# A two-layer encoder on one core: second score products with 128 rows, and a static order made with other costs

## The chip, the core and the metric

The kernel runs on one core of one Trainium2 chip. The metric is the device time of one execution, in microseconds. Three executions of the kernel before were timed; the table further down has them. The profile is of one more execution.

The engines are named as in the profile: PE is TensorE (PEld its weight loads), DVE is VectorE, ACT is ScalarE, POOL is GpSimd, SP is SyncE, which issues the loads and stores.

## The reference

256 tokens of width 1024 pass two layers and a final RMSNorm, all in float32. Cut to what matters:

```python
def hybrid_layer(x, ...):
    proj = rmsnorm(x, n1) @ w_in                       # 1024 -> 2304
    qa, ka, va, qb, kb, vb = jnp.split(proj, cuts, axis=-1)
    qa = axial_rope(rmsnorm(qa, q_norm), ...)          # A: 8 heads of q, 2 of k and v
    ka = axial_rope(rmsnorm(ka, k_norm), ...)
    ya = global_gqa(qa, ka, va)                        # softmax over all 256 keys
    yb = dilated_window_attention(partial_rope(qb), partial_rope(kb), vb)   # B: 8 heads
    y = jnp.concatenate([rmsnorm(ya, out_norm_a), rmsnorm(yb, out_norm_b)], axis=-1)
    x = x + y @ w_out
    u = jnp.square(jax.nn.relu(rmsnorm(x, n2) @ w_mlp_in))   # 1024 -> 4096
    return x + u @ w_mlp_out
```

A head has 64 dims. The three dilated patterns of B merge, on 256 tokens, into one softmax with a mask of logarithms.

## The kernel before, in words

**Products in two parts.** Each float32 operand is split into a part `hi`, rounded to the format that TensorE reads in one pass, and the rest `lo`. A product is then three: hi·hi, hi·lo and lo·hi. The weights come by DMA into a ring `wraw` of 4096 columns (`dma_more`, L468), are split into the rings `whi` and `wlo` of 8192 columns, in pieces of up to 640 (`prep_piece`, L476; `hi` on ACT or DVE, `lo` on DVE, or on DVE or POOL for the weights ahead of the MLP), and are used in the order in which TensorE takes them (`plan`, L35).

**A layer.** q and k of A come first (120 products of 256 columns). Then come the V products (96 of 320 columns), and between them the column sums and transposes that k's and q's norms need (`hook_a0` to `hook_a4`, L676 to L726). The constants in `tabt` (rotary tables, mask) are loaded behind the first weights. Then the 16 heads are run (`score`, `turn`, `pv`, L793 to L840), and the products that don't need them stand between: q and k of B (`fill_pair`, L754) and the A half of the output projection (`fill_wa`, L764). The B half (`fill_wb`), B's norm (`ynorm_col`, `rowbc`), the residual, the second norm and the MLP follow. In layer 1 the sums of the last product start from x, transposed (`seed`, L1002).

**A head's scores** (`score`). q of a head is stationary: its 64 rows of `hi`, and in the other 64 partitions the 64 rows of its `lo`. k's `hi` stands twice, on both halves, so one product of 128 rows gives (q_hi + q_lo)·k_hi. A second product adds q_hi·k_lo, and takes the 64 rows of q_hi alone:

```python
mm(b[:, th], q[:, th * 128:(th + 1) * 128], ks[0], True, False)
mm(b[:, th], q[a, th * 128:(th + 1) * 128], ks[1][a], False, True)
```

This is done for both halves `th` of the tokens: four products of 256 columns a head, 128 in all, 64 of them with 64 rows. In the profile and in the order they are the products that read `qs`, with `ka` for the heads of A and `kbt` for those of B. Behind the scores come, on DVE, the row maximum and small instructions on two numbers a partition (`hst`), on ACT the exponential, and on POOL, DVE or ACT the division by the sum (`pr`); then TensorE transposes `pr` into `h` and `l`, which the P·V products take.

**What sets the order.** Every instruction is recorded by `Sequencer` (L136) and issued from one line, L368, in a static order. `cost` (L191) gives each an assumed duration. `record` (L220) marks which instructions take the SBUF port that DVE and POOL share: DVE's with two SBUF operands, or of the copy and scale kinds from SBUF to SBUF, and POOL's that read SBUF. `order` (L261) is a list schedule over these costs, and `justify` moves all as late, then as early as it can be. `issue` (L361) runs it twice: first with the port, which settles on which engine each instruction runs, then again with engines fixed, and this pass gives the order. In the second pass the marks of the port are left out:

```python
# once with the shared port, for the choice of engines, and once without
self.order()
self.ops = [([x for x in o[0] if x[0] == e], *o[1:5], {}, *o[6:]) for o, e in zip(self.ops, self.on)]
for i in self.order():
```

On the chip each engine keeps its own order and waits on semaphores for the others' results.

Of the kernel before, what the change touches and what calls it, by code (L numbers as in the profile page):

```python
# [10 lines left out]
F32 = mybir.dt.float32  # L11
# [8 lines left out]
NRAW = 4096     # columns of weights as they come  # L20
NHI = 8192      # and split
# [6 lines left out]
NIN0 = 3                              # pairs of ff blocks in the K-outer start of the MLP  # L28
LAG = 2
N_PAIR = 16  # L30
# what an engine's end counts more, in the choice among several, per kind of instruction
# [3 lines left out]
def plan():  # L35
    """The weights in chunks of some columns, in the order in which TensorE takes them."""
    out = []
# [15 lines left out]
def lay_weights(w_in, w_out, w1, w2):  # L53
    """The weights as TensorE takes them: rows of 128 on the partitions, columns
    in the heads' order (kv0 with kv1, first with second of a pair)."""
# [52 lines left out]
def tables():  # L108
    """Constants that depend on shapes alone: rotary cosines and signed sines on
    [dim of two heads, token], the logarithms (times 8) of how many of the dilated  # L110
    patterns a key is in, the identity, and sums over a head or all."""
# [24 lines left out]
class Sequencer:  # L136
    """Takes a kernel's instructions in program order, keeps what that order says
    of their data, and issues them in the order of a list schedule: each engine takes,
    of what is ready for it, what has the longest way to the end."""

    # from the end of one engine's instruction to the start of another's that waits for it
# [21 lines left out]
    def form(e, method, args, kw):  # L163
        """An engine's instruction for what several engines can do."""
# [12 lines left out]
    def regions(ap, psum):  # L177
        """Where an access lies: partitions and spans of the free axis (a whole PSUM bank)."""
# [12 lines left out]
    def cost(e, method, outs, ins, kw):  # L191
# [6 lines left out]
        if e == "PE":  # L198
            f32 = ins[0].dtype == F32
            if kw.get("is_transpose") or method == "transpose":  # L200
                return 109
            return max(110, 1.7 * n) if f32 else max(109, 0.423 * n)
# [17 lines left out]
    def record(self, engines, method, args, kw):  # L220
# [28 lines left out]
        if engines == ("SP",):  # L249
            # the loads in program order  # L250
            if self.last is not None:
                deps.setdefault(self.last, False)
            self.last = i
        # the SBUF port that DVE and Pool share
# [6 lines left out]
    def order(self):  # L261
# [31 lines left out]
        while done < n:  # L293
# [10 lines left out]
            if len(ops[i][0]) > 1:  # L304
                # the engine that ends it first
# [20 lines left out]
    def justify(self, start, end, succ):  # L326
        """Moves all instructions as late as they may be, then as early: gaps close."""
# [3 lines left out]
        for back in (True, False):  # L331
            busy = {e: [] for e in (*self.eng, "PORT")}     # spans, counted from this pass's beginning
# [28 lines left out]
    def issue(self):  # L361
        # once with the shared port, for the choice of engines, and once without
        self.order()
        self.ops = [([x for x in o[0] if x[0] == e], *o[1:5], {}, *o[6:]) for o, e in zip(self.ops, self.on)]
# [15 lines left out]
def trunk(ctx: ExitStack, tc: tile.TileContext, x, wts, prm, tab, fin, out):  # L380
# [19 lines left out]
    # ---------------------------------------------------------------- tiles  # L400
# [21 lines left out]
    KA = [[T(f"ka{i}{s}", [128, S], F32R) for s in range(2)] for i in range(2)]  # L422
# [3 lines left out]
    tq = T("tq", [128, 2, S])             # gain-folded sines of q and k  # L426
    tb = T("tb", [128, 2, S])             # rs-folded tables of B
# [16 lines left out]
    # ------------------------------------------------------------- weights  # L444
# [6 lines left out]
    def places(total):  # L451
        """Each chunk's place in a circular buffer, and the last chunk that it overwrites."""
# [23 lines left out]
    def prep_piece():  # L476
        """Splits a piece of the next chunk, if its place is free."""
# [27 lines left out]
    def wgt(key, a, n, last=True):  # L505
        """(hi, lo) of n columns from a on in a chunk; with `last`, their last use."""
# [17 lines left out]
    # --------------------------------------------------------- small pieces  # L524
    def col(src, rhs, n, o):
        """o[token, th, n] <- column sums of src [128, 256] (weights rhs)."""
        for th in range(2):
            mm(o[:, th], src[:, th * 128:(th + 1) * 128], rhs, True, True)

    def rowbc(c2, o):  # L530
        """o [128, 256] <- c2 [token, th] along the free axis on every partition."""
# [8 lines left out]
    def sums(l, ps):  # L540
        """From column sums of squares of x: mean square + eps, and its power -1/2."""
# [11 lines left out]
    # ---------------------------------------------------------------- start  # L553
    DVE.memset(ssx[:, 0:128], 0.0)
    # TensorE's clock rises while it waits for x
# [10 lines left out]
    DVE.memset(one, 1.0)  # L566
    x3 = x.rearrange("p (a b) -> p a b", a=KB)
# [46 lines left out]
    def norm_x(l):  # L614
        """norm's scale along the tokens, from the squares' sums."""
# [8 lines left out]
    # ---------------------------------------------------------------- layer  # L624
    for l in range(L):
        gA, gA2, gK, gK2 = P(l, 16), P(l, 17), P(l, 18), P(l, 19)
        # gain-folded tables
# [3 lines left out]
        # ---- q and k of A, K-outer behind the split of h  # L631
# [7 lines left out]
        # ---- V of all heads, tokens on the partitions, with the rest of A's q, k between  # L639
# [17 lines left out]
        def k_split(kh, kst_):  # L657
            """kst_[head][hi, lo]: each a head's 64 rows twice."""
# [15 lines left out]
        cq = cqt.rearrange("p (t h) -> p t h", t=2)   # scale of q's scores / 8  # L674
# [78 lines left out]
        # ---- attention of the 16 heads, with the products that don't need it between  # L753
# [324 lines left out]
```

## Time and profile before

| | |
|---|---|
| timed executions | 629.90, 632.05, 635.52 us; median 632.05 |
| span of the profiled execution | 630.3 us (no other time of that execution is known) |
| layer 0: A's q, k and V | to 46.2 us |
| layer 0: 16 heads | 46.2 to 122.0 us |
| layer 0: rest of the projection, second norm | to about 147 us |
| layer 0: MLP | to about 330 us |
| layer 1: 16 heads | 350.8 to 426.2 us |
| layer 1: MLP | from about 458 us |
| DMA | 98.58 MB, mean 156 GB/s |
| mean granted clock of TensorE | 0.992 |

All instructions are recorded by one helper and stand at L368, so the profile is read by tiles: `bank` is PSUM; `whi`, `wlo` the split weights; `hh`, `hl` the normed x; `h`, `l` the transposed softmax or the MLP's inner layer; `sm` and `hst` small columns; `f` scratch. Before the bar of a group's row stand the instruction, its shape and its count; behind it the busy us and the mean ns of one; then the engine's idle time before it. In a timeline's row stand the start, the us from first start to last end, the engine and the instruction with its count. Matmuls overlap each other in the array: what one costs is read from start to start.

### The profile page before, as it was taken

The numbers are of one execution on the slowest core, as the hardware profiler recorded it, in microseconds if no ns is written. First come the engines' busy times: TensorE is split into PE (matmuls) and PEld (weight loads), VectorE is DVE, ScalarE is ACT, GpSimd is POOL, SyncE is SP. The second block draws the span as 40 slices with busy tenths as digits, with TensorE's granted clock in tenths as the row PEclk, the third lists the DMA queues.
The fourth block names the chain that finished last, engine by engine and source line by source line (L and its number), as shares of the span: only waits on it lengthen the run. The fifth ranks groups of instructions, "written<-read, shape, count | busy, mean of one in ns | idle before, by whom it ended". The sixth has DMA issues, their size and how long they took to land.

```text
span 630.3 us, 11899 instructions
## 1 busy us (share of the span) xinstructions
PE 611.6 (97%) x4500; PEld 576.6 (91%) x4500; DVE 483.9 (77%) x873; ACT 353.4 (56%) x723; POOL 181.9 (29%) x179
## 2 busy tenths in 40 slices
PE   8989999989999999999999999999999999999996
PEld 8988987989999999999999888898989999999995
DVE  6898899998986566666588879887988766667632
ACT  6567877865544444434464687786654444434412
POOL 1486885841000000000035766667300000000000
PEclk9979999999999999999999999999999999999999
DMA  7833111346674554645444301025568554544501
GB/s 262 275 150 134 68 68 34 130 139 201 251 251 167 203 186 151 222 177 178 141 151 134 135 35 68 34 74 173 158 242 297 204 205 156 221 180 149 186 1 67
DMA packets 29865, 98.58 MB, mean 156 GB/s; under 512 B 3440, under 2 KB 3952, under 8 KB 29808
## 3 DMA queue, kind: packets, MB, share of 16 engines
q1 hardware_dynamic: 29808, 97.82, 44.3%
q8 instruction: 35, 0.57, 0.3%
q14 instruction: 22, 0.18, 0.1%
HBM read 96.76 MB, written 1.05 MB: 155 GB/s over the span
## 4 chain that ended last, share of the span: by engine, by line
PE 65%; DVE 11%; issue 2%; ACT 1%; POOL 1%; POOLq 0%; ACTq 0%; DVEq 0%
PE bank L368 65%; DVE wlo L368 2%; DVE f L368 2%; DVE hl L368 2%; DVE qs L368 1%; DVE hst L368 1%; DVE xT L368 1%; DVE l L368 1%; DVE pr L368 1%; DVE kbt L368 0%; POOL sm L368 0%; ACT f L368 0%; ACT pr L368 0%; POOL f L368 0%; DVE yA__82 L368 0%
## 5 line engine op out<-in xcount | busy, mean ns | idle before, releaser
L368 ACT ACTIVATE whi<-wraw 128x640 fp32r<-128x640 f32 (+3 forms) x312 | 192.9, 643 | 171.3 <-PE bank L368 113.0
L368 DVE TENSOR_TENSOR wlo<-wraw,whi 128x640 fp32r<-128x640 f32 (+3 forms) x296 | 221.0, 777 | 64.7 <-ACT whi L368 63.5
L368 PE MATMUL bank<-hh,whi 128*128 128x256 f32 x784 | 222.4, 285 | 0.7 <-ACT whi L368 0.7
L368 PE MATMUL bank<-hl,whi 128*128 128x256 f32 x784 | 222.5, 285 | 0.6 <-DVE hl L368 0.5
L368 PE MATMUL bank<-hh,wlo 128*128 128x256 f32 x784 | 221.2, 285 | 0.1
L368 PEld LDWEIGHTS bank<-hh,whi 128*128 128x128 f32 x784 | 149.2, 191 | 2.4 <-ACT whi L368 1.2
L368 PEld LDWEIGHTS bank<-hl,whi 128*128 128x128 f32 x784 | 148.1, 189 | 1.4 <-DVE hl L368 1.2
L368 PEld LDWEIGHTS bank<-hh,wlo 128*128 128x128 f32 x784 | 147.3, 189 | 0.6 <-DVE wlo L368 0.3
L368 POOL TENSOR_TENSOR wlo<-wraw,whi 128x384 fp32r<-128x384 f32 (+1 forms) x49 | 66.8, 1375 | 161.1 <-DMA wraw<-in_w_dram 149.7
L368 PE MATMUL bank<-l,whi 128*128 128x256 f32 x256 | 72.4, 283 | 0.0
L368 PE MATMUL bank<-h,wlo 128*128 128x256 f32 x256 | 72.2, 282 | 0.0
L368 PE MATMUL bank<-h,whi 128*128 128x256 f32 x256 | 71.3, 280 | 0.0
L368 POOL TENSOR_TENSOR sm<-sm,mhalf 128x2 f32<-128x2 f32 (+2 forms) x12 | 11.8, 986 | 183.8 <-DVE sm L368 183.8
L368 PE MATMUL bank<-wlo,h 128*128 128x512 f32 (+1 forms) x160 | 56.1, 350 | 0.0
L368 PE MATMUL bank<-whi,l 128*128 128x512 f32 (+1 forms) x160 | 55.9, 349 | 0.0
L368 PE MATMUL bank<-whi,h 128*128 128x512 f32 (+1 forms) x160 | 55.8, 349 | 0.0
L368 PEld LDWEIGHTS bank<-h,whi 128*128 128x128 f32 x256 | 48.4, 190 | 0.0
L368 PEld LDWEIGHTS bank<-h,wlo 128*128 128x128 f32 x256 | 48.0, 188 | 0.0
L368 PEld LDWEIGHTS bank<-l,whi 128*128 128x128 f32 x256 | 47.9, 187 | 0.1
L368 POOL TENSOR_TENSOR ssx<-ssx,f 128x512 f32<-128x512 f32 (+1 forms) x22 | 27.6, 1253 | 48.7 <-ACT f L368 37.3
L368 ACT ACTIVATE h<-f 128x512 fp32r<-128x512 f32 x32 | 20.2, 631 | 28.1 <-DVE f L368 28.1
L368 DVE CAST whi<-wraw 128x640 fp32r<-128x640 f32 (+1 forms) x33 | 14.8, 452 | 26.9 <-PE bank L368 25.6
(113 smaller groups left out, 994.8 us busy)
## 6 DMA issues: line engine op xcount, KB each, us to landing
wraw<-in_w_dram SPq DMA_DIRECT2D x148, 512.0 KB, 3.7
wraw<-in_w_dram SPq DMA_DIRECT2D x31, 320.0 KB, 3.3
wraw<-in_w_dram SPq DMA_DIRECT2D x16, 384.0 KB, 3.3
tabt<-in_t_dram SPq DMA_DIRECT2D x1, 768.0 KB, 7.5
xT<-in_x_dram SPq DMA_DIRECT2D x1, 512.0 KB, 7.0
tabt<-in_f_dram SPq DMA_DIRECT2D x1, 512.0 KB, 7.0
out_dram<-f SPq DMA_DIRECT2D x1, 512.0 KB, 2.6
out_dram<-f SPq DMA_DIRECT2D x2, 256.0 KB, 2.2
```

Source lines behind the costliest of these rows:

```text
L368: getattr(self.eng[e], method)(*args, **kw)
```

## The change

Three things change. The second score product takes all 128 rows: `ks[1]` is read whole, and its other half is zeroed once at the start (four memsets on POOL), so that q's `lo` rows are multiplied by zero. The four tiles of A's k become one tile, `ka`. The planner's cost of a product rises from 0.423 ns a column (at least 109) to 4 + 0.449 ns (256 columns: 109 to 119; 320: 135 to 148; 512: 217 to 234). And the second scheduling pass keeps the marks of the port.

```diff
@@ cost
-            return max(110, 1.7 * n) if f32 else max(109, 0.423 * n)
+            return max(110, 1.7 * n) if f32 else max(109, 4 + 0.449 * n)
@@ issue
-        self.ops = [([x for x in o[0] if x[0] == e], *o[1:5], {}, *o[6:]) for o, e in zip(self.ops, self.on)]
+        self.ops = [([x for x in o[0] if x[0] == e], *o[1:]) for o, e in zip(self.ops, self.on)]
@@ trunk
-    KA = [[T(f"ka{i}{s}", [128, S], F32R) for s in range(2)] for i in range(2)]
+    KAt = T("ka", [128, 2, 2, S], F32R)
+    KA = [[KAt[:, i, s] for s in range(2)] for i in range(2)]
...
     DVE.memset(one, 1.0)
+    for i in range(2):
+        b = slice(64 - 64 * i, 128 - 64 * i)
+        POOL.memset(KAt[b, i, 1].bitcast(F32), 0.0)
+        POOL.memset(KBt[b, :, i, 1].bitcast(F32), 0.0)
@@ score
-            a = slice(64 * (k % 2), 64 * (k % 2) + 64)
             b = v2(bank[k % 2])
             for th in range(2):
-                mm(b[:, th], q[:, th * 128:(th + 1) * 128], ks[0], True, False)
-                mm(b[:, th], q[a, th * 128:(th + 1) * 128], ks[1][a], False, True)
+                for s in range(2):
+                    mm(b[:, th], q[:, th * 128:(th + 1) * 128], ks[s], s == 0, s == 1)
```

The rest of the diff removes comments. The number of instructions hardly changes: PE 4454 and 4454, DVE 861 and 863, ACT 656 and 655, POOL 184 and 187 (four of them the memsets). Both versions issue the same loads in the same order. The new costs and marks move instructions on every engine, and a few between engines: over both layers DVE gets three more rotary products with `tb` and two more of the sums behind them, which POOL loses.

**VectorE in layer 0's V products**, from the tables' first use to k's scaling, which reads PSUM bank 7 (`bank_70`). `sm` in the copy is k's scale, `f<-f,tq` and `f<-f` are q's rotary products. Before:

```order
L368 COPY f_101<-sm_116 128x256
L368 SCALAR_TENSOR_TENSOR f_101<-bank_66,prmt,tabt 128x256
L368 SCALAR_TENSOR_TENSOR f_101<-bank_63,prmt,tabt 128x512
L368 TENSOR_TENSOR f_101<-f_101,tq 128x512
L368 TENSOR_TENSOR f_101<-f_101 128x512
L368 TENSOR_TENSOR wlo<-wraw,whi 128x640
L368 TENSOR_TENSOR f_101<-bank_70,f_101 128x256
```

and now:

```order
L368 SCALAR_TENSOR_TENSOR f_98<-bank_63,prmt,tabt 128x512
L368 SCALAR_TENSOR_TENSOR f_98<-bank_66,prmt,tabt 128x256
...
L368 TENSOR_TENSOR f_98<-f_98,tq 128x512
...
L368 TENSOR_TENSOR f_98<-f_98 128x512
L368 TENSOR_TENSOR wlo<-wraw,whi 128x640
L368 TENSOR_TENSOR qs_83<-f_98,qs_83 64x512
L368 COPY f_98<-sm_113 128x256
L368 TENSOR_TENSOR qs_84<-f_98,qs_84 64x512
L368 TENSOR_TENSOR wlo<-wraw,whi 128x640
L368 TENSOR_TENSOR f_98<-bank_70,f_98 128x256
```

The copy stood ahead of the tables' first use and now stands behind q's rotary products and a split. On TensorE the column sums of q's first heads and the two transposes of the copy stood behind 36 of the 96 V products, and the column sums of q's other heads behind 60; now these three stand behind 48, 70 and 85. All of them write bank 7, which k's scaling reads.

**GpSimd in layer 1's attention**, at its beginning. `pr` is a head's division by its sum, `wlo` a weight piece. Before:

```order
L368 TENSOR_SCALAR pr_103<-pr_103,hst 128x256
L368 TENSOR_SCALAR pr_104<-pr_104,hst 128x256
L368 TENSOR_TENSOR wlo<-wraw,whi 128x640
L368 TENSOR_SCALAR pr_102<-pr_102,hst 128x256 x2
L368 TENSOR_SCALAR pr_103<-pr_103,hst 128x256
L368 TENSOR_TENSOR f_101<-f_101,tb 128x512
L368 TENSOR_TENSOR f_101<-f_101 128x512
L368 TENSOR_SCALAR pr_104<-pr_104,hst 128x256 x2
```

and now:

```order
L368 TENSOR_SCALAR pr_100<-pr_100,hst 128x256
L368 TENSOR_TENSOR wlo<-wraw,whi 128x384
L368 TENSOR_SCALAR pr_101<-pr_101,hst 128x256 x2
L368 TENSOR_TENSOR wlo<-wraw,whi 128x384
L368 TENSOR_TENSOR wlo<-wraw,whi 128x640
L368 TENSOR_SCALAR pr_99<-pr_99,hst 128x256
L368 TENSOR_TENSOR wlo<-wraw,whi 128x384
L368 TENSOR_TENSOR wlo<-wraw,whi 128x640
L368 TENSOR_TENSOR wlo<-wraw,whi 128x384
```

Between the first and the last `pr` of layer 1, POOL had 9 weight pieces and now has 17; in layer 0 it had 14 and now has 18. DVE has 4 instead of 2 there in layer 1, and 2 instead of 3 in layer 0. On TensorE a head's score, transposes and P·V products stand further apart, with more other products between.

**VectorE behind layer 1's attention**: `sm<-bank` begins the scale of B's outputs, `f<-bank,bcr` multiplies the projection's sums by it, `xT<-f,xT` is the residual sum. Before:

```order
L368 TENSOR_SCALAR sm_113<-bank_63 128x2
L368 TENSOR_TENSOR wlo<-wraw,whi 128x768 x2
L368 TENSOR_TENSOR f_101<-bank_64,bcr_107 128x256 x2
L368 TENSOR_TENSOR xT<-f_101,xT 128x256 x2
L368 TENSOR_TENSOR f_101<-bank_68,bcr_107 128x256
L368 SCALAR_TENSOR_TENSOR hl<-xT,prmt,hh 128x256
L368 TENSOR_TENSOR wlo<-wraw,whi 128x768
```

and now:

```order
L368 TENSOR_SCALAR sm_110<-bank_63 128x2
L368 SCALAR_TENSOR_TENSOR hl<-yt_103,prmt,hh 128x256
L368 TENSOR_TENSOR f_98<-bank_64,bcr_104 128x256 x2
L368 TENSOR_TENSOR f_98<-bank_68,bcr_104 128x256 x2
L368 TENSOR_TENSOR f_98<-bank_69,bcr_104 128x256 x2
L368 TENSOR_TENSOR xT<-f_98,xT 128x256 x4
L368 SCALAR_TENSOR_TENSOR hl<-xT,prmt,hh 128x256 x4
```

Six instructions that read PSUM now stand together, ahead of four sums that read SBUF alone. On TensorE, between B's last column sum and the transposes of its scale, stood 19 products in layer 0 and 33 in layer 1; now it is 40 and 23. Behind the transposes, two of layer 1's 16 seed transposes stood after 24 products, the others over 130 later; now eight stand after 16 to 19 products.

## The prediction

> **What bounds the kernel now.** I read the page first, then a table by stage, then the timelines of the engines in the stages that stood out.
>
> ```profile
> span 630.3 us, 11899 instructions
> PE 611.6 (97%) x4500; PEld 576.6 (91%) x4500; DVE 483.9 (77%) x873; ACT 353.4 (56%) x723; POOL 181.9 (29%) x179
> PE 65%; DVE 11%; issue 2%; ACT 1%; POOL 1%; POOLq 0%; ACTq 0%; DVEq 0%
> ```
>
> TensorE is busy for 97% of the span and carries most of the chain that ended last; VectorE is second on that chain. A busy TensorE need not run at its best rate, so the next view is a table of stages: the attention of layer 0 (first score product to last P·V product), that of layer 1, and 100 us of layer 0's MLP. Behind each engine stands its busy time and, in brackets, its instructions.
>
> ```profile
> core 0: us, PE busy (x) PEld busy (x) DVE busy (x) ACT busy (x) POOL busy (x), PEclk, DMA share, GB/s
> 46.20:122.00 75.80, 73.79 (x516) 64.63 (x515) 68.97 (x157) 61.57 (x162) 56.43 (x63) 1.00 0.22 78
> 350.80:426.20 75.40, 73.42 (x507) 63.98 (x506) 64.08 (x151) 59.34 (x159) 50.49 (x57) 1.00 0.21 75
> 200.00:300.00 100.00, 100.00 (x836) 100.00 (x835) 65.98 (x104) 41.43 (x70) 0.00 (x0) 1.00 0.52 183
> ```
>
> In the MLP a product of 256 columns starts every 100/836 = 0.120 us. In the attention 516 products take 75.8 us, 0.147 us each, though many are 128-column transposes, and the granted clock is 1.00. TensorE is hardly idle there (2.0 us of each stage), so it works slowly. Where, shows its timeline around three heads (x4 is one head's score: two first products of 128 rows, each followed by a second one of 64):
>
> ```profile
> 69.17 1.22 PE L368 MATMUL bank<-ka,qs 128*128 128x256 f32 x4
> 70.31 0.66 PE L368 MATMUL bank<-idt,pr 128*128 128x128 f32 x4
> ...
> 79.17 1.21 PE L368 MATMUL bank<-kbt,qs 128*128 128x256 f32 x4
> 80.32 0.39 PE L368 MATMUL bank<-h,V 128*128 128x256 f32 x1
> ```
>
> ```profile
> 359.03 1.21 PE L368 MATMUL bank<-ka,qs 128*128 128x256 f32 x4
> 360.18 0.39 PE L368 MATMUL bank<-hh,whi 128*128 128x256 f32 x1
> ```
>
> From the start of a head's four products to the start of what follows pass 1.14 to 1.15 us; four products at the MLP's pace would take 0.48 us. So a score loses 0.67 us, without any wait.
>
> **The change part by part.**
>
> (1) *The second score products with 128 rows.* 64 products of the 128 change from 64 rows to 128; none is added. If they then keep the pace of their neighbours, 32 heads gain 32 x 0.67 = 21.4 us, 10.7 us in each layer, all of it on TensorE, which is at work or pacing others throughout. Bounds: nothing, if a product takes its 0.3 us for another reason than its rows; 21.4 us, if all goes.
>
> [...]
>
> (2) *What the faster TensorE asks of VectorE.* In layer 0's attention VectorE is busy 68.97 us; TensorE without the 10.7 us needs 75.8 - 10.7 = 65.1 us. VectorE would not fit. In layer 1 it is 64.08 against 64.7. What can go is VectorE's waiting for GpSimd at the port:
>
> ```profile
> 92.57 1.26 DVE L368 TENSOR_TENSOR qs<-f,qs 64x256 fp32r<-64x256 f32 x1
> 93.86 1.13 DVE L368 TENSOR_SCALAR hst<-hst 128x2 f32<-128x2 f32 x1
> ...
> 96.20 0.41 DVE L368 TENSOR_TENSOR kbt<-f,kbt 64x256 fp32r<-64x256 f32 x1
> ...
> 96.61 0.14 DVE L368 TENSOR_SCALAR hst<-hst 128x2 f32<-128x2 f32 x1
> ...
> 97.37 0.42 DVE L368 TENSOR_TENSOR qs<-f,qs 64x256 fp32r<-64x256 f32 x1
> ```
>
> ```profile
> 92.00 1.55 POOL L368 TENSOR_TENSOR wlo<-wraw,whi 128x640 fp32r<-128x640 f32 x1
> 93.51 1.46 POOL L368 TENSOR_TENSOR f<-f,tb 128x512 f32<-128x512 f32 x1
> ```
>
> The same instruction takes 0.42 us alone and 1.26 us beside a GpSimd instruction, one on two numbers 0.14 or 1.13 us. The means of such groups (the number ahead of the last bar, in ns) show how much that is in all, and price what moves:
>
> ```profile
> L368 DVE TENSOR_TENSOR wlo<-wraw,whi 128x640 fp32r<-128x640 f32 x162 | 142.7, 899 | 56.7 <-ACT whi L368 56.5
> ...
> L368 DVE TENSOR_TENSOR f<-f 128x512 f32<-128x512 f32 x37 | 28.4, 773 | 0.4
> ...
> L368 DVE TENSOR_TENSOR qs<-f,qs 64x256 fp32r<-64x256 f32 x16 | 11.0, 688 | 0.5
> ...
> L368 DVE TENSOR_TENSOR kbt<-f,kbt 64x256 fp32r<-64x256 f32 x16 | 9.9, 618 | 0.3
> ...
> L368 DVE TENSOR_SCALAR hst<-hst 128x2 f32<-128x2 f32 x16 | 7.3, 454 | 0.2
> ...
> L368 DVE SCALAR_TENSOR_TENSOR hl<-yt,prmt,hh 128x256 fp32r<-128x256 f32 x8 | 7.1, 898 | 0.1
> L368 DVE SCALAR_TENSOR_TENSOR yA__82<-yt,prmt,yA__82 128x256 fp32r<-128x256 f32 x8 | 6.9, 870 | 0.0
> ```
>
> Against 0.42, 0.41, 0.14 and 0.47 us alone (the last two; row at 430.72 below), the lower five wait 16 x 0.27 + 16 x 0.21 + 16 x 0.31 + 8 x 0.43 + 8 x 0.40 = 19.3 us in both layers, 9.6 us in each attention. The new order keeps the port in its second pass, so it puts VectorE's PSUM work beside GpSimd's; but every engine only keeps its own order and nothing holds the two together in time. I take half of the waits as gone: 4.8 us a layer (bounds 0 and 9.6). The reassignment puts five rotary products (0.77 us) back on VectorE, 1.9 us a layer, takes one weight piece (0.9 us) from it in layer 0's attention and gives it two in layer 1's. So VectorE needs 68.97 - 4.8 + 1.0 = 65.2 us in layer 0, and 64.08 - 4.8 + 3.7 = 63.0 in layer 1. It now reaches 91% in layer 0's attention; taking 94%, since TensorE will wait for it more often, the stages last 69.4 and 67.0 us. That is 4.3 and 2.3 us above the 65.1 and 64.7 of TensorE alone: **+6.6 us** (bounds 0, if all port waits go, and 16.7, if none does). Late next are the split weights that TensorE fills the stage with; SyncE's loads keep their order and are not late (DMA share 0.22).
>
> (3) *Layer 0's V products.* Here TensorE stalls, and then runs at half its clock:
>
> ```profile
> 28.87 0.95 PE L368 MATMUL bank<-idt,f 128*128 128x2 f32 x8
> 30.60 0.44 PE L368 MATMUL bank<-idt,f 128*128 128x128 f32 x2 [0.78 <-DVE f L368]
> ...
> 36.66 1.64 PE L368 MATMUL bank<-idt,f 128*128 128x2 f32 x8 [2.10 <-DVE f L368]
> ```
>
> ```profile
> 37.00:43.00 6.00, 6.00 (x25) 5.96 (x25) 5.80 (x11) 5.40 (x11) 4.40 (x3) 0.50 0.27 91
> ```
>
> ```profile
> 31.17 1.14 DVE L368 SCALAR_TENSOR_TENSOR f<-bank,prmt,tabt 128x256 f32<-128x256 f32 x2 [0.63 <-DMA tabt<-in_t_dram]
> ...
> 34.57 1.61 DVE L368 TENSOR_TENSOR wlo<-wraw,whi 128x640 fp32r<-128x640 f32 x1
> 36.10 0.41 DVE L368 TENSOR_TENSOR f<-bank,f 128x256 f32<-128x256 f32 x1
> ```
>
> The column sums at 36.66 wait for bank 7, which k's scaling reads at 36.10, behind a weight piece stretched to 1.61 us. The clock is then 0.50 for the 6 us from 37 on, worth 3 us. Now the transposes of k's scale stand 34 V products (5.0 us) later, and the 15 products behind them, 2.2 us, cover the three VectorE instructions up to the scaling. But these transposes now wait for work that starts when the tables land (31.17): two products (1.14), two more for q (2 x 0.77), a piece (0.9), a q split and the copy (estimated like these, 0.8 and 0.7) and some 0.4 of small ones: 36.6. TensorE is there at 29.8 + 5.0 = 34.8. One stall of 1.8 us takes the place of 0.78 + 2.10: -1.1; whether the clock falls again I take as even: -1.5. Together **-2.6 us** (bounds -6, if all goes, and +1).
>
> [...]
>
> (4) *The scale of B's outputs, and the seeds.* From B's last column sum to the transposes of its scale passes a chain over VectorE and GpSimd:
>
> ```profile
> 429.20 0.36 PE L368 MATMUL bank<-idt,f 128*128 128x1 f32 x2
> 433.46 0.38 PE L368 MATMUL bank<-idt,sm 128*128 128x128 f32 x2
> ...
> 438.23 0.33 PE L368 MATMUL bank<-idt,xT 128*128 128x128 f32 x1 [1.08 <-DVE xT L368]
> ```
>
> ```profile
> PE bank L368 <- POOL sm L368: 2.5, 2, 1.6
> ```
>
> ```profile
> 430.72 0.47 DVE L368 SCALAR_TENSOR_TENSOR hl<-yt,prmt,hh 128x256 fp32r<-128x256 f32 x1
> ```
>
> The chain takes 4.3 us. Layer 0 now has 40 products (4.8 us) between instead of 19: its wait of 1.6 us goes. Layer 1 has 23 (2.7 us) instead of 33: a wait of 1.6 us comes. In layer 1 eight seed transposes instead of two are asked for early, and two of VectorE's sums more must be there: +1 us. Together **+1.0 us** (0 to 3).
>
> (5) *GpSimd's four memsets* stand ahead of its first sum of squares, where it is idle; nothing follows from them. Were it not idle, they would cost about the 0.6 us of its shortest passes over 256 columns, each. The planner's longer matmul (119 for 256 columns, which the trace shows as 0.120) moves instructions, and is counted in what moved.
>
> Sum against the profiled span: 630.3 - 21.4 + 6.6 - 2.6 + 1.0 = 613.9. The median run, 632.05, is 1.75 us above that span, so the time is **615.7 us**.
>
> **The rivals.**
>
> *VectorE and the port keep the attention (B).* GpSimd gets 17 weight pieces instead of 9 in layer 1's attention (18 instead of 14 in layer 0), each holding the port. If no port wait goes, VectorE needs 68.97 + 1.0 and 64.08 + 3.7 us; at 94% the stages last 74.4 and 72.1 us, 10.1 us above (2)'s. Time 625.8. For it speaks that VectorE is already busy 91%; against, that the old order ignored the port and the new one does not. A milder form, 621, lies between.
>
> *All waits go (C).* No new wait in attention, no stall and no half clock in the V products: 632.05 - 21.4 - 6 = 604.6. For it: the new order spreads a head's score, transposes and P·V further apart. Against: VectorE's 65.2 us of work in 65.1.
>
> *The widening does nothing (D).* A second product takes its time for another reason than its rows, and keeps it. TensorE then asks no more of VectorE, and (3) and (4) alone act: 632.05 - 2.6 + 1.0 = 630. Against it: a head's first and second products read the same q into the same bank, and other products with 128 rows start every 0.12 us. [...]
>
> *GpSimd falls behind: slower (E).* GpSimd is in order, and each head's softmax scaling there stands behind weight pieces.
>
> ```profile
> L368 POOL TENSOR_TENSOR wlo<-wraw,whi 128x384 fp32r<-128x384 f32 x32 | 38.9, 1222 | 11.3 <-DVE whi L368 6.6 <-ACT whi L368 4.8
> ```
>
> If each of 32 heads waits one piece more on TensorE, 1.22 us, that is 39 us less the 16.4 of the forecast: 655; it is slower than before from 0.51 us a head, and 640 at 0.76. Against: 5 to 12 us of other products stand between a score and its transposes.
>
> **How the numbers follow.** Forecast 0.60, B 0.20, C 0.11, D 0.04, E 0.05. The likeliest is 615.7. Range 603 to 627: it holds C's and B's figures and leaves out D and E. A change of 1% (6.3 us) is about what a measurement of this kernel tells from none. Faster by more: forecast, C and most of B, 0.88; within: D and the rest of B, 0.07; slower: 0.05.
>
> **What would show it.** Right: four score products in about 0.48 us; attention stages of 66 to 70 us at VectorE 92 to 96%; the instructions on q and k nearer to 0.42; the half clock gone or shorter. Wrong: score products still at 0.3 us (D); stages above 72 us with TensorE waiting for l, hl or weights (B); TensorE waiting for GpSimd's pr (E).

## The result and the profile after

The changed kernel takes 622.75 us (median of 4 runs, 621.07 to 624.57) against 630.98 us for the kernel before on the same chip: a ratio of 0.985 with a 95% interval of 0.981 to 0.988. It is 8.2 us faster where 16.4 were forecast; the time lies in the range, near the milder form of rival B (621).

From the page of the profiled execution, the span, the busy shares, and the chain of work that ended last by engine:

```profile
span 622.2 us, 11915 instructions
PE 596.8 (96%) x4500; PEld 575.3 (92%) x4500; DVE 459.3 (74%) x875; ACT 352.5 (57%) x722; POOL 175.7 (28%) x182
PE 79%; DVE 10%; DMA 4%; ACT 4%; issue 1%; SPq 1%; POOL 0%; POOLq 0%; ACTq 0%; DVEq 0%
```

VectorE is busy for 24.6 us less than before (483.9) with two instructions more: the excess at the port (its measure stands under the table of the parts) fell from 54.1 to 25.7 us. The table by stage, over the same three stages as before (columns as there):

```profile
core 0: us, PE busy (x) PEld busy (x) DVE busy (x) ACT busy (x) POOL busy (x), PEclk, DMA share, GB/s
44.89:120.87 75.98, 69.07 (x522) 65.87 (x520) 64.89 (x159) 63.78 (x166) 54.23 (x60) 0.93 0.22 72
352.17:421.25 69.08, 66.04 (x524) 63.99 (x523) 60.97 (x156) 60.51 (x158) 48.52 (x60) 0.98 0.30 98
200.00:300.00 100.00, 100.00 (x836) 100.00 (x835) 66.62 (x106) 41.88 (x70) 0.00 (x0) 1.00 0.54 182
```

Layer 1's attention went from 75.4 to 69.1 us. Layer 0's lasts 76.0 us, where it lasted 75.7: there TensorE is now 69 us at work instead of 74, at a mean clock of 0.93. The scores themselves, on TensorE's timeline:

```profile
62.88 0.63 PE L368 MATMUL bank<-ka,qs 128*128 128x256 f32 x4
63.35 0.28 PE L368 MATMUL bank<-hl,whi 128*128 128x256 f32 x1
...
63.70 0.71 PE L368 MATMUL bank<-ka,qs 128*128 128x256 f32 x4
64.25 0.28 PE L368 MATMUL bank<-hl,whi 128*128 128x256 f32 x1
```

From the start of a head's four products to the start of what follows pass 0.47 to 0.55 us instead of 1.15. So the rows did what they were to do. In layer 0 the gain was given back as waits. The view of TensorE's waits lists those of the whole kernel by what ended them (us in total, times, longest):

```profile
PE bank L368 <- ACT hh L368: 3.2, 1, 3.2
PE bank L368 <- DVE f L368: 2.4, 2, 1.8
PE bank L368 <- DVE kbt L368: 1.9, 1, 1.9
...
PE bank L368 <- DVE l L368: 1.5, 2, 1.0
PE bank L368 <- DVE hst L368: 1.4, 1, 1.4
...
PE bank L368 <- DVE yA__82 L368: 1.0, 1, 1.0
```

Several of these have a stretch at half clock near them. The table by stage over the four longest such stretches:

```profile
31.50:38.50 7.00, 7.00 (x30) 7.00 (x30) 5.36 (x8) 3.09 (x6) 5.32 (x5) 0.52 0.34 105
86.00:96.50 10.50, 8.58 (x41) 8.23 (x39) 8.53 (x30) 8.06 (x21) 5.42 (x8) 0.51 0.05 15
133.50:137.00 3.50, 3.50 (x18) 3.39 (x18) 3.50 (x9) 3.12 (x7) 0.00 (x0) 0.55 0.00 0
392.50:396.50 4.00, 3.41 (x17) 3.41 (x17) 3.81 (x10) 3.18 (x9) 0.27 (x1) 0.60 0.00 0
```

In these stretches the clock is at half for some 24 us, where the kernel before had 7.

To see where the gain went I add up, over TensorE's instructions, the time from the start of one to the start of the next beyond its best pace (0.119 us for 256 columns, 0.147 for 320, 0.234 for 512, 0.109 for a transpose). What stands at a change between 64 and 128 rows is counted as "rows", all else (waits and half clock) as "waits". The difference of the two sums is the difference of the spans, 8.1 us:

| lost by TensorE, us | to the first score | attention 0 (rows + waits) | 40 us behind it | attention 1 (rows + waits) | the rest |
|---|---|---|---|---|---|
| before | 12.0 | 11.1 + 4.3 | 3.1 | 11.4 + 4.6 | 5.5 |
| after | 10.6 | 0 + 15.0 | 6.3 | 0 + 7.7 | 4.2 |
| change | -1.4 | -0.4 | +3.2 | -8.3 | -1.3 |
| forecast | -2.6 | -6.4 | -1.6 | -8.4 | +2.6 |

Layer 1's attention came out as forecast. Layer 0's gave all of its 11 us back, and the residual behind it has a new stall. The first column hangs on the single execution more than on the order, as (3) below shows.

### The profile page after: what moved, and what is told of

It reads as the page before. It is cut to its first block, busy times and chain, and to the rows that moved or that the text cites. A ratio compares the mean times of both kernels' runs of the same rounds, so it can differ in the third digit from the quotient of the medians.

```text
span 622.2 us, 11915 instructions
## 1 busy us (share of the span) xinstructions
PE 596.8 (96%) x4500; PEld 575.3 (92%) x4500; DVE 459.3 (74%) x875; ACT 352.5 (57%) x722; POOL 175.7 (28%) x182
## 4 chain that ended last, share of the span: by engine, by line
PE 79%; DVE 10%; DMA 4%; ACT 4%; issue 1%; SPq 1%; POOL 0%; POOLq 0%; ACTq 0%; DVEq 0%
PE bank L368 79%; DMA wraw<-in_w_dram 4%; DVE f L368 2%; DVE wlo L368 2%; DVE l L368 1%; DVE hst L368 1%; ACT pr L368 1%; DVE pr L368 1%; DVE yt L368 1%; DVE kbt L368 1%; ACT f L368 1%; ACT whi L368 1%; SPq L368 1%; DVE qs L368 1%; DVE hl L368 1%
## 5 line engine op out<-in xcount | busy, mean ns | idle before, releaser
L368 DVE TENSOR_TENSOR wlo<-wraw,whi 128x640 fp32r<-128x640 f32 (+3 forms) x294 | 212.8, 753 | 71.5 <-ACT whi L368 70.2
L368 PEld LDWEIGHTS bank<-hh,whi 128*128 128x128 f32 x784 | 147.6, 189 | 5.8 <-ACT hh L368 3.5
L368 PEld LDWEIGHTS bank<-hh,wlo 128*128 128x128 f32 x784 | 148.9, 191 | 1.4 <-DVE wlo L368 1.3
L368 POOL TENSOR_TENSOR wlo<-wraw,whi 128x384 fp32r<-128x384 f32 (+1 forms) x51 | 63.6, 1262 | 149.2 <-DMA wraw<-in_w_dram 145.5
L368 PEld LDWEIGHTS bank<-h,whi 128*128 128x128 f32 x256 | 47.8, 188 | 0.0
L368 POOL TENSOR_TENSOR ssx<-ssx,f 128x512 f32<-128x512 f32 (+1 forms) x22 | 29.1, 1322 | 61.4 <-ACT f L368 50.9
L368 PEld LDWEIGHTS bank<-wlo,h 128*128 128x128 f32 x160 | 30.2, 189 | 4.4
## 6 DMA issues: line engine op xcount, KB each, us to landing
out_dram<-f SPq DMA_DIRECT2D x2, 256.0 KB, 2.2
```

Source lines behind the costliest of these rows:

```text
L368: getattr(self.eng[e], method)(*args, **kw)
```

## The experiments

The question was where layer 0's 11 us went: into the order, the clock, or another engine. The theories' numbers start anew with each group of runs. All times are medians; ratios are to the kernel before, run beside each kernel.

**The parts by themselves.** Theory 1 is here the forecast's own mechanism, Theory 2 that the new order eats the gain. The first four kernels keep some of the three edits. Against the changed kernel:

```
e1  -  max(109, 4 + 0.449 * n)      +  max(109, 0.423 * n)
    -  (..., *o[1:])                +  (..., *o[1:5], {}, *o[6:])
e2  second products on q[a], ks[1][a] (64 rows), no zeros
e3  -  (..., *o[1:])                +  (..., *o[1:5], {}, *o[6:])
e4  -  max(109, 4 + 0.449 * n)      +  max(109, 0.423 * n)
```

> Only the wider second products (with the zeros they need); the planner keeps its old price of a matmul and drops the port in its second pass, so the order is made as before. Theory 1 (the rows bring the gain, but VectorE's waits at the port have to fall before TensorE can use it): VectorE still needs about 69 us in layer 0's attention and 64 in layer 1's; at 94% busy the two stages last 73 and 68 us instead of 75.7 and 75.4, about 621 us, 619 to 624. Theory 2 (the new order is what eats the gain, through its stalls of 1.9 and 3.2 us and the half clock behind them): the stages come near TensorE's own 65 us, 66 to 67 each, and the time is 614 or less.

> Only the planner's two edits (port kept in the second pass, longer matmul); the second score products keep 64 rows. Theory 1: a head's four products still take 1.15 us, VectorE's waits at the port fall but it is not what TensorE waits for, so 627 to 633, no change. Theory 2: the new order brings its stalls and the half clock along, 635 or more. If the order rather than the rows had brought the gain: 625 or less.

> Wider rows and the longer matmul, without the port in the second pass. Theory 1: VectorE's excess at the port stays near the 54 us of before, and the time is that of the rows alone within 2 us. Theory 2: the stalls of the new order come from the port marks, so this kernel has them not and takes 614 or less.

> Wider rows and the port in the second pass, with the old price of a matmul. Theory 1: the excess at the port is halved as in the whole change, near 26 us, and the time is 618 to 624, at or below that of the rows alone. Theory 2: the marks bring the long stalls, the clock falls to half for more than 15 us in all, and the time is above that of the rows alone.

| kernel | time, us | ratio (95%) | attention 0 and 1, us | waits of TensorE there, us | VectorE's excess at the port, us |
|---|---|---|---|---|---|
| before | 631 to 633 | 1 | 75.7, 75.4 | 4.3, 4.6 | 54.1 |
| e1 rows | 623.90 | 0.985 (0.980 to 0.991) | 75.7, 71.4 | 15.3, 12.1 | 55.3 |
| e2 order (price and port) | 638.28 | 1.009 (1.005 to 1.013) | 85.6, 76.5 | 15.5, 4.3 | 25.7 |
| e3 rows and price | 638.09 | 1.010 (1.006 to 1.013) | 73.5, 75.6 | 13.9, 16.1 | 54.7 |
| e4 rows and port | 631.49 | 0.997 (0.994 to 1.000) | 78.1, 67.8 | 17.7, 14.1 | 36.3 |
| after: all three | 622.75 | 0.985 (0.981 to 0.988) | 76.0, 69.1 | 15.0, 7.7 | 25.7 |

(The excess is the sum, over VectorE's instructions that overlap one of GpSimd's, of their time beyond the shortest of the same form. Differences of a few tens of ns are left out; with them every row is some 3 to 4 us higher. "The port" is the kernel's own word, from `record`; what the traces show is the lengthening. In the kernel before, the splits of q took 0.69 us on average against 0.42 alone, and the scalings of two numbers 0.45 against 0.14, while instructions that read PSUM kept theirs beside GpSimd, as the sum `yt<-bank,f` with 0.42 us on average and 0.43 at most.)

The wider rows alone bring what the whole change brings. The two edits of the planner together cost 0.9% without the rows and bring nothing measurable with them. Each of the two alone, put on the rows, makes the kernel slower: by 14 us (price) and 8 us (port). So the parts don't add, and an order alone moves the time by up to some 2%. Theory 1 held for e1's time alone (623.9, with layer 0 at 75.7 instead of 73) and missed e2, e3 and e4. Theory 2 is right for e2 and e4 (whose clock is at half for some 27 us), wrong for e1 and e3.

The order-only kernel shows most. Its layer 0 attention in the table by stage:

```profile
40.14:125.77 85.63, 80.39 (x522) 69.63 (x520) 63.74 (x159) 64.03 (x166) 54.18 (x60) 0.92 0.20 65
```

Its scores are still slow, by some 9 us in this stage, and yet TensorE loses some 15 us on top, about 11 more than in the old order and as much as in the changed kernel. (Where a stall and a change of rows fall on one instruction, the split between the two is an estimate; their sum is 24.6 us.) It stalls in front of the same instructions as the changed kernel: the second score product with `kbt`, the product with `yA`, the transposes of `pr`, the P·V product with `l` and, behind the stage, the first product of the MLP. These waits do not come from TensorE's being faster; they stand in the order.

The old order with the wider rows has a different bound in the same place:

```profile
41.96:117.62 75.66, 67.42 (x516) 64.40 (x515) 71.37 (x159) 61.27 (x162) 59.30 (x64) 0.95 0.26 84
346.51:417.92 71.41, 64.65 (x507) 62.00 (x506) 64.40 (x151) 58.87 (x158) 50.79 (x57) 0.98 0.25 76
```

Here VectorE is busy for 71.4 of 75.7 us, 94%: what rival B described, all waits at the port included. The new order takes those away (64.9 us) and puts as long a stage in their place. Layer 0's attention lasts 73.5 to 78.1 us in all four kernels with the wider rows.

**Is it the clock?** Theory 1 is now that the stalls let the clock fall and that the half clock is the loss; Theory 2, that VectorE or GpSimd sets the pace, so that TensorE would wait anyway. Products of the identity ahead of stalled instructions keep TensorE at work:

```
+            if e == "PE":
+                n, o = FILL.get(at, (0, None))
+                for _ in range(n):
+                    fo = args[0] if o is None else self.bank[o][:, 128:256]
+                    self.eng[e].matmul(fo[:, :128], self.ident, self.ident, ...)
+                at += 1
```

> The changed kernel with its order unchanged, and 39 extra products of the identity (0.22 us each at full clock) put ahead of seven of TensorE's instructions that stall (2 at 28 us, 7 at 83, 2 at 88, 5 at 90, 3 at 110, 13 at 130, 7 at 391): they fill the stalls, so that TensorE is not idle, and their results are overwritten or never read. Theory 1 (about 24 us at half clock, 12 us lost, follow from the stalls): the clock stays at 1.00 behind the filled stalls, layer 0's attention shrinks from 76.0 to about 71 us, and the time is 613 to 617. Theory 2 (VectorE or GpSimd sets that stage's pace, and what the clock takes TensorE would wait for anyway): the clock stays up, new waits take its place, 620 to 624.

Measured: 620.52 us, ratio 0.982 (0.975 to 0.989). The seven products at 83 us turned out to stand ahead of a head's second score product, so they are added to the diagonal of one half of its scores; this changes the output, not the work. Layer 0's attention, and the ten microseconds that had run at half clock:

```profile
42.77:118.79 76.02, 69.97 (x556) 66.28 (x554) 65.28 (x159) 63.85 (x166) 54.35 (x60) 1.00 0.23 72
86.00:96.00 10.00, 7.24 (x53) 6.36 (x53) 8.39 (x24) 8.57 (x23) 5.38 (x7) 1.00 0.18 52
```

The clock is 1.00 throughout, and the stage is as long as before, 76.0 us. Five of the added products came behind a wait instead of in it (their bank was still read by VectorE) and cost 1.1 us; so the clock's own share of this stage is about 1.1 us at most, not 5. Theory 1 falls: at full clock TensorE only arrives earlier at the same waits.

> The same in the kernel with the wider rows alone and the old order: 41 extra products of the identity ahead of six stalled instructions (12 at 46 us, 4 at 77, 7 at 100, 5 at 124, 7 at 350, 6 at 384). In it the clock is at half from 48 to 54, 102 to 108 and 352 to 356 us, some 8 us lost. Theory 1: the clock stays up there and the time falls from 623.9 to 616 to 619. Theory 2: waits take its place, 622 to 625.

Measured: 628.61 us, ratio 0.993 (0.990 to 0.996), 5 us slower than e1. This test failed as built:

```profile
50.67 2.94 PE L376 MATMUL bank<-idt 128*128 128x128 f32 x24 [2.94 <-ACT pr L379]
```

The twelve products (two records each) write the bank whose reader the stalled instruction waited for, so they wait as long (2.94 us) and then run on top of it. It tells nothing of the clock.

**Is it GpSimd, or VectorE?** Of the changed kernel's 15.0 us of waits in layer 0, 9.9 lie between 82 and 100 us. Its table by stage there, and ahead of it:

```profile
76.00:82.00 6.00, 5.68 (x43) 4.94 (x41) 4.92 (x19) 5.76 (x16) 2.79 (x6) 1.00 0.00 0
82.00:92.00 10.00, 6.20 (x35) 5.63 (x34) 9.80 (x24) 8.77 (x27) 4.92 (x6) 0.70 0.15 53
92.00:100.00 8.00, 6.88 (x39) 6.48 (x39) 6.14 (x18) 6.26 (x17) 6.14 (x6) 0.73 0.38 125
```

VectorE, 85% busy over the stage, is 98% busy in the ten microseconds in which TensorE has little to do, and 77% in the eight behind. Within them VectorE's timeline, GpSimd's and TensorE's read:

```profile
82.23 1.43 DVE L368 TENSOR_SCALAR hst<-hst 128x2 f32<-128x2 f32 x2
83.69 1.72 DVE L368 TENSOR_TENSOR kbt<-f,kbt 64x256 fp32r<-64x256 f32 x1
```

```profile
82.35 1.28 POOL L368 TENSOR_TENSOR f<-f 128x512 f32<-128x512 f32 x1
83.59 1.53 POOL L368 TENSOR_TENSOR wlo<-wraw,whi 128x640 fp32r<-128x640 f32 x1
```

```profile
85.46 0.62 PE L368 MATMUL bank<-kbt,qs 128*128 128x256 f32 x3 [1.88 <-DVE kbt L368]
```

The split of k, 0.41 us alone, ends 0.3 us behind GpSimd's weight piece, 1.72 us after its start, and TensorE waits 1.88 us for it. Two kernels take work from GpSimd and from VectorE, in the unchanged order:

```
e7   +  if e == "POOL" and "out" in kw and kw["out"].tensor.name == self.lo:
     +      kw = {k: v[:, :64] if hasattr(v, "tensor") else v for k, v in kw.items()}
e12  +  the same on DVE, where out is l and in0 is in PSUM
```

> The changed kernel in its order, but each of GpSimd's 51 splits of weights writes 64 of its 384 or 640 columns, so that it holds the port for a sixth to a tenth of the time (the rest of the low parts stays what an earlier piece left there, or zeros written once by VectorE at the start). If GpSimd's pieces make layer 0's stalls, by holding the port or by being late themselves: the waits of 1.9 us at 83, 1.4 at 90 and 3.2 at 130 us shrink below 0.7 us, the stage falls from 76.0 to about 68 us and the time is 608 to 614. If the stalls are the length of the chains over VectorE and ScalarE in that order: stalls and time stay, 619 to 624.

> The changed kernel in its order, with less work on VectorE in the attention: of the 32 low parts of the transposed probabilities (128x512, 0.69 us each), 28 are made for 64 of their 512 columns only, 12 in layer 0 and 16 in layer 1; the other columns stay what an earlier one left, so the output is not the reference's. VectorE has some 6.6 us less to do in layer 0's attention and 8.8 in layer 1's; TensorE, ScalarE and GpSimd have the same to do. If VectorE's own work in that order sets the pace (the term of the forecast on VectorE, too small as it was): layer 0's attention shrinks from 76.0 to 71 us or less and layer 1's from 69.1 towards 65.5, and the time is 613 to 617. If the chains over ScalarE and GpSimd set it: the waits change their name, the stage stays above 74 us, and the time is 619 to 623.

Measured: e7 614.87 us, ratio 0.974 (0.967 to 0.9805); e12 618.83 us, ratio 0.980 (0.976 to 0.983). The attention stages of e7, then of e12:

```profile
42.22:115.20 72.98, 66.74 (x522) 63.58 (x520) 60.66 (x159) 63.49 (x166) 35.27 (x62) 0.98 0.24 78
346.08:412.87 66.79, 64.26 (x524) 62.32 (x523) 58.81 (x155) 60.21 (x158) 30.68 (x59) 1.00 0.33 104
```

```profile
40.36:114.54 74.18, 67.19 (x522) 64.22 (x520) 60.48 (x159) 63.57 (x166) 54.29 (x61) 0.95 0.24 74
345.30:412.79 67.49, 65.09 (x524) 63.54 (x523) 53.85 (x156) 60.31 (x158) 49.41 (x59) 0.97 0.32 99
```

e7 lands between its two expectations; e12 comes near its second, with layer 0's stage above 74 us, though TensorE's waits there still end with VectorE. With 19 us less of GpSimd's work layer 0's attention gains 3.0 us, and with 18 less layer 1's gains 2.3; with 4.4 us less of VectorE's, layer 0's gains 1.8. In e7 the wait for `kbt` is gone, but at 84 and 88 us stand waits of 1.75 and 1.86 us for ScalarE instead; the stall behind the stage, 3.2 us at 130 us in the changed kernel, is still 3.2 us. In e12 the same stretch shows why little came of it:

```profile
79.00:88.00 9.00, 5.56 (x28) 5.01 (x29) 8.17 (x23) 8.41 (x26) 3.52 (x5) 0.69 0.13 49
```

VectorE is at 91% and ScalarE at 93%, GpSimd at 39%. So neither VectorE alone nor GpSimd alone bounds these ten microseconds: VectorE, part of whose time is its wait at the port, and ScalarE are both nearly full there, and when one is relieved the other stays. No run takes work from ScalarE, so how much of the stage it holds is open.

**What the 64 rows cost.** This kernel is the one before, with one line moved:

```
 for th in range(2):
-    mm(b[:, th], q[...], ks[0], True, False)
-    mm(b[:, th], q[a, ...], ks[1][a], False, True)
+    mm(b[:, th], q[...], ks[0], th == 0, False)
+for th in range(2):
+    mm(b[:, th], q[a, ...], ks[1][a], False, True)
```

> The kernel before, with 64-row second products, but a head's two first products (128 rows) come ahead of its two second ones (64 rows): TensorE goes from 128 to 64 rows and back 64 times instead of 128, with the same 64 products of 64 rows. If the loss of 22.5 us is paid at each change of the row count (0.176 us each): a head's four products take about 0.8 us instead of 1.15, TensorE's own time falls by 11 us, and the time by 3 to 9. If it is paid for each product of 64 rows: 1.15 us as before, and 629 to 634.

Measured: 624.92 us, ratio 0.989 (0.984 to 0.994). Its scores on TensorE's timeline:

```profile
69.33 0.91 PE L368 MATMUL bank<-ka,qs 128*128 128x256 f32 x4
70.17 0.38 PE L368 MATMUL bank<-hh,whi 128*128 128x256 f32 x1
...
78.82 0.91 PE L368 MATMUL bank<-kbt,qs 128*128 128x256 f32 x4
79.66 0.38 PE L368 MATMUL bank<-hh,whi 128*128 128x256 f32 x1
```

A head takes 0.84 us: of the 0.67 us above 0.48, about half is gone with half of the changes. In this kernel, then, the loss is paid for changing the row count, not for a product of 64 rows. The ends of the single products, which the profile models, say the same: a head's two second products end 0.117 us apart, like two first ones, and the steps at which the row count changes take 0.31 us. And this half of the gain on TensorE brings 1.1%, about what all of it brings in e1 (1.5%, with overlapping intervals), one more sign that the rest stops at other engines: layer 0's attention again lasts 76.0 us, VectorE busy for 73.4 of them:

```profile
44.69:120.74 76.05, 69.98 (x521) 63.57 (x520) 73.42 (x159) 62.30 (x162) 59.62 (x64) 1.00 0.27 87
```

**Mending the order by hand.** One kernel halves GpSimd's pieces, one changes the order of the residual. The stall at 130 us lies behind this row on VectorE, with the row on TensorE that waits:

```profile
124.50 5.76 DVE L368 TENSOR_TENSOR wlo<-wraw,whi 128x768 fp32r<-128x768 f32 x4
130.18 2.06 DVE L368 TENSOR_TENSOR f<-bank,bcr 128x256 f32<-128x256 f32 x6
132.17 1.08 DVE L368 TENSOR_TENSOR xT<-f,xT 128x256 f32<-128x256 f32 x3
```

```profile
133.23 0.62 PE L368 MATMUL bank<-hh,whi 128*128 128x256 f32 x3 [3.16 <-ACT hh L368]
```

The three kernels with the port marks (e2, e4, after) have the block of six and a stall of 3.2 to 3.7 us there; the three without (before, e1, e3) have products and sums nearly in turn, and no stall above 0.4 us at that instruction.

```
e9   -  tensor_tensor(out=wlo, in0=wraw, in1=whi)     +  the same on each half of the columns
e10  -  f f f f f f xT xT xT                          +  f xT f xT f xT f f f
```

> The changed kernel in its order and with all its work, but each of GpSimd's 51 splits of weights is issued as two instructions of half the columns. If it is the length of one stretch at the port that hurts (a VectorE instruction on two numbers waits 1.1 to 1.4 us for the end of a GpSimd piece in the chain that TensorE waits for): such an instruction waits for half as long, the excess on VectorE falls from 25.7 to about 18 us, layer 0's attention from 76.0 to 74 and the time from 622.75 to 618 to 621. If it is the sum of GpSimd's time at the port, or its lateness: the second instruction's fixed part adds to it, 622 to 626.

> The changed kernel with one thing moved by hand in both layers: the six products of the B sums with their scale, which the port marks put ahead of the first addition to x, now alternate with the additions (product, addition, product, addition). If that block of six makes the stall of 3.2 us at 130 us: the first normalised block is ready some 1.6 us earlier, the stall falls to 1.6 us or less, the half clock behind it (134 to 137 us) goes or gets shorter, and the time is 619 to 621. If something else is late there (the weight splits ahead of it, or GpSimd's additions to x): the stall stays above 2.5 us and the time 622 to 624.

> The two together. The two lie in different places (attention, and the residual behind it), so their gains should add: 615 to 619 if both help; if each change of the order only moves the stalls elsewhere, 621 to 625.

Measured: e9 624.74 us, ratio 0.9885 (0.9845 to 0.9925); e10 626.43 us, 0.991 (0.9875 to 0.995); e11 625.83 us, 0.990 (0.986 to 0.994). None is faster than the changed kernel. In e9 the excess at the port did not fall (28.1 us), and VectorE's instructions on two numbers still take 441 ns on average (490 in the changed kernel, 140 alone). In e10 the stall only split in two:

```profile
129.25 0.62 PE L380 MATMUL bank<-hh,whi 128*128 128x256 f32 x3 [2.47 <-ACT hh L380]
131.50 0.58 PE L380 MATMUL bank<-hl,whi 128*128 128x256 f32 x1 [1.63 <-DVE hl L380]
```

ScalarE makes weight splits until 128.8 us, so the first `hh` comes 0.7 us earlier instead of 1.6, and the low parts `hl`, still behind three products, are late next. In layer 1 the same exchange opens a stall. The seed transposes waited 1.0 us in the changed kernel; in e10 they wait 0.6 and then 2.1 us, and half clock follows from 434 to 437 us:

```profile
432.18 0.44 PE L380 MATMUL bank<-idt,xT 128*128 128x128 f32 x2 [2.12 <-DVE f L380]
```

So the block of six is at most a part of layer 0's stall. The larger part can be read from TensorE's order around the transposes of B's scale, before and now:

```profile
129.72 0.43 PE L368 MATMUL bank<-idt,sm 128*128 128x128 f32 x2 [1.60 <-POOL sm L368]
```

```profile
129.10 0.38 PE L368 MATMUL bank<-idt,sm 128*128 128x128 f32 x2
```

Between B's last column sum and the MLP's first product stand 45 products in both. Before, 19 of them stood ahead of these transposes and 26 behind; now it is 40 and 5. From the transposes to the first `hh` passed 2.9 us, which 26 products covered. Now it is 4.1 us, and five products cover 0.6 of them. All three kernels with the stall have five products there, and the three without it 24 to 26. The longer chain is at most 1.2 us of the 3.2; the rest is the cover that went to the front. No run moves the products back, so this is read from the traces and not tested.

## Why the prediction was right, and where it was wrong

**(1), the second products: right.** 22.5 us of TensorE's own time went (21.4 forecast), in e1, e3 and e4 too. The rival that the widening does nothing is out.

The time fell into the range, which was drawn wide enough to hold rival B. The gain is half of the forecast's: the terms were off by +6.0 us in layer 0's attention, +4.8 behind it, +1.2 ahead of it and -3.9 in the rest. That these partly cancel is luck.

**(2), what TensorE then asks of VectorE: this is the step that failed, and only in layer 0.** VectorE's work was forecast well: 65.2 and 63.0 us, measured 64.9 and 61.0. About half of the excess at the port went, as taken, though unevenly (the groups of the prediction's list, ahead of the last bar their mean in ns):

```profile
L368 DVE TENSOR_TENSOR qs<-f,qs 64x256 fp32r<-64x256 f32 x16 | 8.1, 507 | 0.5
...
L368 DVE TENSOR_SCALAR hst<-hst 128x2 f32<-128x2 f32 x16 | 7.4, 490 | 0.0
...
L368 DVE SCALAR_TENSOR_TENSOR yA__82<-yt,prmt,yA__82 128x256 fp32r<-128x256 f32 x8 | 4.0, 504 | 0.0
```

The splits of q (688 before) and yA (870) came nearer to their 420 and 470 alone; the instruction on two numbers (454) did not. The failure is "at 94%" for a whole stage. VectorE reaches 85% in layer 0 and 88% in layer 1, since its work is bunched: 98% for the ten microseconds in which the first pairs of B are split while A's last heads and the first WA products run, 77% right after. The stage came out 6.6 us longer than the 69.4 forecast. Layer 1's is 2.1 us longer than forecast, but it holds 17 products (2 us) more than before, and by TensorE's losses the term is right (-8.3 against -8.4). e2 shows that layer 0's loss is the new order's, since TensorE loses as much there with slow scores; e5 that it isn't the clock; e7 and e12 that it is neither GpSimd nor VectorE alone. Which chain of that order holds the stage is not shown further.

Read again, the profile of before had it: TensorE 97% busy at a slow pace and VectorE 91% busy filled the same 75.7 us. Speeding up the one leaves the other's length, as e1 shows with 75.7 us. Rival B, at 74.4 us for this stage, was near in its number only: its cause, port waits that stay, is e1's and not the changed kernel's.

**(3), the V products: size not shown.** In the profiled execution the two stalls became 0.75 and 0.45 us, less than the 1.8 forecast, and 1.4 us were gained instead of 2.6, because the half clock came all the same. But e2, e10 and e12 have the same instructions in the same order up to the first score, and reach it at 40.1, 41.4 and 40.4 us, the changed kernel at 44.9. In nearly the old order the first score comes at 46.3 us (before), 42.0 (e1) and 44.7 (e8). So executions of one order differ by more than this term. "Even odds" was fair: of the seven kernels with this order, e5 with its filled stalls aside, four fell to half clock in the V products. e12 has a clock of 1.00 and 85 of TensorE's instructions in the twelve microseconds where the changed kernel has 0.72 and 56. The changed kernel, then e12:

```profile
28.00:40.00 12.00, 10.80 (x56) 10.30 (x55) 8.52 (x15) 6.06 (x11) 8.01 (x10) 0.72 0.56 186
```

```profile
28.00:40.00 12.00, 11.52 (x85) 11.51 (x86) 9.91 (x20) 8.03 (x16) 9.11 (x10) 1.00 0.54 161
```

**(4), B's scale and the seeds: mis-sized in both directions.** Layer 0's wait of 1.6 us went, as forecast. But the 21 products that fill it came from behind the transposes, where they had covered the chain to the MLP's first product; the prediction put that at nothing. Nor did it follow VectorE's order there, where six products now stand ahead of the first sum. The result is a stall of 3.2 us and a half clock behind it, +3.2 instead of -1.6. In layer 1 the wait of 1.6 us that was to come did not, and the seeds' wait is 1.0 us as it was, so that the rest gained 1.3 us where 2.6 were to be lost.

**(5), the memsets, and the longer matmul:** the memsets show nowhere, as forecast. The longer matmul "moves instructions, and is counted in what moved" was too light: alone on the rows it costs 14 us, with the port marks it makes the order some 8 us better (e3 against e1, after against e4). Why is open; the runs show only that the planner's picture and the chip part so far that an order made with better figures is not a better order.

## What to carry to other kernels

An engine that is busy for a whole stage at a slow pace can hide a second bound of the same length: before pricing a speedup, cut the stage into pieces of some ten microseconds and ask of each which engines are full there; an average of 85% had 98% in it. When a static order is remade, time the order by itself with the old work: here it cost 0.9%, and the whole change was worth no more than its first part alone. When products are moved to fill a wait, ask what they covered where they stood. A half clock behind a stall is not its price by itself: fill the stall once and see whether the stage gets shorter.

## What the runs showed of the hardware

In the kernel before, changing the row count cost TensorE about 0.18 us each time, 22.5 us over 128 changes. Half of the changes, in e8, cost about half: a head's four products took 0.84 us there, against 1.15 before and 0.47 with 128 rows throughout. By the ends that the profile models, a second product of 64 rows took as long as a first one of 128 where it stood behind another of 64 (0.117 us in e8), and 0.31 us wherever the row count changed.

The half clock followed no length of stall: it came behind two of 0.75 and 0.45 us (29 and 31 us in the changed kernel), behind one of 1.9 us (85 us there) and behind one of 2.1 us (36.7 us in the kernel before), and did not come behind one of 1.6 us (129.7 us in the kernel before) nor behind one of 2.1 us (52 us in e8, where the clock is 1.00 from 46 to 62 us). The same instructions ran at half clock in one kernel and at full clock in another: from 28 to 40 us the mean clock is 0.72 in the changed kernel and 1.00 in e12. In the changed kernel's four stretches the half clock lasts 6.83, 10.24, 3.41 and 3.41 us, and the full clock between them 47.8, 37.5 and 256.0 us. What starts and ends such a stretch no run shows.
